# Hybrid decoder trunk on one core: the MLP's up and down products issued in pairs of one kind

## The chip, the cores and the metric

The kernel runs on one core of one Trainium2 chip. The time is that of one execution on the device, in microseconds; lower is better. The core has a matrix engine (TensorE, PE in the profile, with its weight loads shown apart as PEld), three engines for elementwise work (VectorE or DVE, ScalarE or ACT, GpSimd or POOL) and a queue that starts transfers (SyncE, SP). TensorE writes its results to PSUM, eight banks of 128 x 512 floats here, from which DVE and ACT read them.

## The reference

Two layers on a residual stream of 512 tokens by 1024, in float32. The first has a latent attention, the second a gated linear attention, and each is followed by an MLP:

```python
def sq_relu_mlp(xn, w_up, w_down):
    hid = jnp.square(jax.nn.relu(xn @ w_up))
    return hid @ w_down

def reference(x, ...):
    for i in range(DEPTH):              # DEPTH = 2
        xn = rms_norm(x, norm_mix[i])
        ...                             # mixer
        x = x + mix.astype(x.dtype)
        x = x + sq_relu_mlp(rms_norm(x, norm_mlp[i]), mlp_w_up[i], mlp_w_down[i]).astype(x.dtype)
    return rms_norm(x, final_norm)
```

`w_up` is 1024 x 4096, `w_down` 4096 x 1024. Only the MLP is touched by the change.

## The kernel before

Each float32 operand is split into a high part, which ACT copies, and a low part, which DVE subtracts; a product is then three matmuls (high by high, high by low, low by high). The split of a weight piece of 128 x 1024 is `piece`: `wh` on ACT (L104), `wl` on DVE (L107). There are four rooms for `wh` and four for `wl`, so a piece is split at the earliest when the product four places before it has left its room.

`mlp` walks over the 4096 hidden columns in eight blocks of 512. Its first up block is done plainly (`up_first`); then come seven calls of `step(b)`, b = 0 to 6, and the last down block stands behind them. A step multiplies down block b and up block b+1, both by a scheme with seven products of half-size blocks in place of eight (sums of quadrants are formed before and after). So a step has seven up products and seven down products:

- an up product (`up_product`, matmuls on L946) is 24 matmuls, each with a 128 x 128 block of split weights held in the array and 256 columns of activations moving; it writes one bank of the tag `u` (four of them: `z`, `y`, `w`, `w2`);
- a down product (`down_product`, matmuls on L955) is 12 matmuls, each with a 128 x 128 block of activations held and 512 columns of weights moving; it writes two banks, `d` or `e`, of which there is one pair each.

Up products are named by their quadrant: 11, 21, T2, T1, 22, T3, T4. In before, they alternate with the down products: up 11, down `d11`, up 21, down `d12`, up T2, down `d11` (changed in place by `ds1`, against -q11), up T1, down `d12` (changed in place), up 22, down `ds3`, up T3, down `ds1`, up T4, down `d22`.

Around the products stand the sums. ACT copies a bank into another as the start of the next sum (`begun`, L964; L976 and L978 in `onto`), DVE adds banks to totals (L1000, L971), and `finish` squares the hidden values of the next block (DVE L849, ACT L850). The quadrants q11, q12, q21, q22 are changed in place on DVE (L1002, L1003, L1034, L1045).

Weights come by DMA. `fetch` starts the transfer of the next block's piece as soon as `after(name)` is called, that is when this block's piece of that room has been used: `A1` and `A2` are the up pieces (1 MB each, rooms `wraw`, started on SP at L134), `S1`, `dS1`, `dS3`, `d11`, `d12`, `d22` the others (rooms `comb`, L933). A second transfer from POOL's queue adds a further quadrant to `S1`, `dS1`, `dS3` and `A2` (L935, L925). A transfer waits on its queue until the room is free, and those behind it wait with it.

The framework's scheduler turns the program into one row of instructions per engine. On PE that row follows the program's order in all steps but b = 0, and ACT, DVE and SP follow it with small shifts.

Of the kernel before, what the change touches and what calls it, by code (L numbers as in the profile page):

```python
# [14 lines left out]
AF = mybir.ActivationFunctionType  # L15
ALU = mybir.AluOpType
# [34 lines left out]
def trunk_kernel(ctx: ExitStack, tc: tile.TileContext, t_in: dict, out: bass.AP):  # L51
    nc = tc.nc
    PE, ACT, DVE, POOL, SP = nc.tensor, nc.scalar, nc.vector, nc.gpsimd, nc.sync
# [5 lines left out]
    def uname(s):  # L59
        count[0] += 1  # L60
        return f"{s}_{count[0]}"
# [14 lines left out]
    def bank(tag):  # L76
        return psum["pool"].tile([P, 512], F32, tag=f"ps_{tag}", bufs=psum["banks"][tag], name=uname("ps"))

    def two_banks(tag):
        return psum["pool"].tile([P, 1024], F32, tag=f"ps_{tag}", bufs=1, name=uname("ps2"))  # L80

    def split_banks(tag):
        t = two_banks(tag)
        return [t[:, :512], t[:, 512:]]
# [4 lines left out]
    def tmp(shape=(P, 512), dt=F32):  # L89
        return sb.tile(list(shape), dt, tag="tmp", bufs=6, name=uname("tmp"))  # L90
# [11 lines left out]
    def split(src, hi, lo, hi_eng=ACT, lo_eng=DVE, order=lambda i: i):  # L102
        if hi_eng is ACT:
            order(ACT.activation(hi, src, AF.Copy))  # L104
        else:
            hi_eng.tensor_copy(hi, src)
        lo_eng.tensor_tensor(lo, src, f(hi), ALU.subtract)  # L107
# [35 lines left out]
    def piece(raw, a, n, order=lambda i: i, at=W_AT):  # L143
        hi = room_for("wh", a, n, at)
        lo = room_for("wl", a, n, at)
        split(raw, hi, lo, order=order)
        return hi, lo

    def cut(pair, *idx):
        return tuple(t[idx] for t in pair)  # L150
# [654 lines left out]
    def mlp(layer, nrm, nxt=None):  # L805
        w_up, w_dn = t_in["mlp_w_up"][layer], t_in["mlp_w_down"][layer]
        X = nrm.out
        NB = FF // FB
# [13 lines left out]
        S11, S12, SU, S21, S5 = sums  # L822
# [7 lines left out]
        def by_tile(v):  # L830
            return v.rearrange("p (j t) -> p j t", j=2)

        def signed(src, hi, lo, sign):
            ACT.activation(hi, src, AF.Copy, scale=sign)
            DVE.scalar_tensor_tensor(lo, src, sign, f(hi), ALU.mult, ALU.subtract)

        def parts_of_quad(src, sign=1.0):
            hi, lo = parts_room[turn[0] % 4]
            turn[0] += 1
            if sign == 1.0:  # L840
                split(src, hi, lo)
            else:
                signed(src, hi, lo, sign)
            return hi, lo

        def finish(src, half, th, q):
            r = tmp()
            r_t = nrm.rstd[:, (first, second)[th]].unsqueeze(1).to_broadcast([P, 2, TH])
            DVE.scalar_tensor_tensor(by_tile(r), by_tile(src), 0.0, r_t, ALU.min if half else ALU.max, ALU.mult)  # L849
            ACT.activation(q[half][th], r, AF.Square)  # L850
# [87 lines left out]
        def up_product(t, a, q, start):  # L938
            w = piece(a, KH, 256, at=W_AT_UP)
            for j in range(2):  # L940
                o = t[:, j * TH : (j + 1) * TH]
                for k in range(KH):
                    wh, wl = cut(w, slice(None), k, slice(j * P, (j + 1) * P))
                    xh, xl = quad[q][k][:, 0], quad[q][k][:, 1]
                    for n, (a_, x_) in enumerate(((wh, xh), (wh, xl), (wl, xh))):
                        PE.matmul(o, a_, x_, start=start and j == 0 and k == 0 and n == 0, stop=k == KH - 1 and n == 2, skip_group_check=True)  # L946

        def down_product(t, a, parts, start):
            wh, wl = piece(a, 2, 512)
            for tt in range(2):  # L950
                o = t[:, tt * 512 : (tt + 1) * 512]
                for k in range(2):
                    xh, xl = cut(parts, slice(None), slice(k * TH + tt * P, k * TH + (tt + 1) * P))
                    for n, (x_, w_) in enumerate(((xh, wh[:, k]), (xh, wl[:, k]), (xl, wh[:, k]))):
                        PE.matmul(o, x_, w_, start=start and k == 0 and n == 0, stop=k == 1 and n == 2, skip_group_check=True)  # L955


        def step(b, q, r, after):
            opening = b == 0 and nxt is not None
            (q11, q12), (q21, q22) = q  # L960

            def begun(src):
                t = two_banks("e")
                ACT.activation(t, src, AF.Copy)  # L964
                return t

            def add(total, t):
                if opening:
                    ACT.activation(total, t, AF.Copy)
                else:  # L970
                    DVE.tensor_tensor(total, t, total, ALU.add)  # L971

            def onto(tag, total, a, parts, fresh=False):
                t = two_banks(tag)
                if not fresh:
                    ACT.activation(t, total, AF.Copy)  # L976
                down_product(t, a, parts, fresh)
                ACT.activation(total, t, AF.Copy)  # L978

            A1, A2, s1 = W["A1"], W["A2"], W["S1"]  # L980
            a11, a12, s3, a22 = A1[:, :KH], A1[:, KH:], A2[:, :KH], A2[:, KH:]
            d11, d12, ds1, ds3, d22 = (W[n] for n in ("d11", "d12", "dS1", "dS3", "d22"))

            z = bank("u")
            up_product(z, a11, "11", True)
            y = bank("u")
            ACT.activation(y, z, AF.Copy)

            d = two_banks("d")
            down_product(d, d11, parts_of_quad(q11), True)  # L990
            if opening:
                ACT.activation(S11, d, AF.Copy)
            e = two_banks("e") if opening else begun(d)

            up_product(y, a12, "21", False)
            finish(y, 0, 0, r)
            DVE.tensor_tensor(a11, s1, a11, ALU.add)

            down_product(e, d12, parts_of_quad(q21), opening)
            DVE.tensor_tensor(S11, e, S11, ALU.add)  # L1000
            DVE.tensor_tensor(d11, ds1, d11, ALU.add)
            DVE.tensor_tensor(q12, q22, q12, ALU.subtract)  # L1002
            DVE.tensor_tensor(q11, q11, q12, ALU.add)  # L1003

            up_product(z, a11, "T2", False)
            u = tmp()
            ACT.activation(u, z, AF.Copy)
            DVE.tensor_tensor(a12, a11, a12, ALU.add)

            down_product(d, d11, parts_of_quad(q11, -1.0), False)  # L1010
            e = begun(d)
            DVE.tensor_tensor(d12, d11, d12, ALU.add)
            after("d11")

            w = bank("u")
            up_product(w, s1, "T1", True)
            w2 = bank("u")
            ACT.activation(w2, w, AF.Copy)
            after("S1")

            down_product(e, d12, parts_of_quad(q22), False)
            add(S12, e)
            after("d12")

            up_product(w, a12, "22", False)
            c = tmp()
            DVE.tensor_tensor(c, w, u, ALU.add)
            finish(c, 0, 1, r)
            after("A1")

            down_product(d, ds3, parts_of_quad(q12), False)
            add(SU, d)
            after("dS3")
            DVE.tensor_tensor(q22, q22, q11, ALU.subtract)  # L1034

            up_product(z, s3, "T3", False)
            v = tmp()
            ACT.activation(v, z, AF.Copy)
            c = tmp()
            DVE.tensor_tensor(c, w2, v, ALU.add)  # L1040
            finish(c, 1, 1, r)

            onto("e", S5, ds1, parts_of_quad(q22, -1.0), b == 0)
            after("dS1")
            DVE.tensor_tensor(q21, q21, q11, ALU.subtract)  # L1045

            up_product(z, a22, "T4", False)
            finish(z, 1, 0, r)
            after("A2")

            onto("d", S21, d22, parts_of_quad(q21, -1.0), opening)
            after("d22")

        up_first(Q[0])
        quadrants()
# [45 lines left out]
        for b in range(NB - 1):  # L1101
# [3 lines left out]
            def after(name, b=b, final=final, old=old):  # L1105
                if final:
                    return before_next(name) if nxt else at_the_end(name)
                new = NEXT[name]
                if name in home:
                    home[new] = old[name]  # L1110
                fetch(b + 1, new)
# [4 lines left out]
        if nxt:  # L1116
# [6 lines left out]
            for c in range(2):  # L1123
                if c == 0:
                    ps_ = [bank("u") for _ in range(4)]
                else:
                    e, d = split_banks("e"), split_banks("d")
# [6 lines left out]
                for j, p in enumerate(ps_):  # L1134
                    if j % 2 == 0:
                        w = piece(last_raw[c][:, :, j * P : (j + 2) * P], 4, 256)
# [524 lines left out]
    for k0, k1 in ((0, 1), (1, 2), (2, 4), (4, 6), (6, 8)):  # L1661
        w = piece(raw0[:, k0:k1], k1 - k0, KL, tc.keep_in_program_order)
# [9 lines left out]
    O, begun = mla(0, nrm, w0, mla_pools)  # L1672
# [23 lines left out]
    Y, begun = gla(0, n_mix1, "B", "B")  # L1696
# [54 lines left out]
```

## Time and profile before

| what | value |
|---|---|
| runs shown, median of 3 | 1054.07 us (1053.84 to 1054.35) |
| profiled execution | 1054.16 us |
| its span, first to last instruction | 1052.4 us |
| TensorE busy | 1043.0 us (99%) |
| VectorE busy | 874.2 us (83%) |
| ScalarE busy | 702.6 us (67%) |
| granted TensorE clock | 0.999 |

A profile row of an instruction gives its start and length in us (the length runs to the end of the last matmul of a group, and neighbouring matmuls overlap in the pipe, so the rate of PE is read from the distance of the starts), then the engine, the line, the operation, what it writes and reads with the sizes, and how many are taken together. In brackets stands how long the engine was idle before it and who ended that. The chain of waits goes back from the last instruction to what released each one.

### The profile page before, as it was taken

The numbers are of one execution on the slowest core, as the hardware profiler recorded it, in microseconds if no ns is written. First come the engines' busy times: TensorE is split into PE (matmuls) and PEld (weight loads), VectorE is DVE, ScalarE is ACT, GpSimd is POOL, SyncE is SP. The second block draws the span as 40 slices with busy tenths as digits, with TensorE's granted clock in tenths as the row PEclk, the third lists the DMA queues.
The fourth block names the chain that finished last, engine by engine and source line by source line (L and its number), as shares of the span: only waits on it lengthen the run. The fifth ranks groups of instructions, "written<-read, shape, count | busy, mean of one in ns | idle before, by whom it ended". The sixth has DMA issues, their size and how long they took to land.

```text
span 1052.4 us, 15648 instructions
## 1 busy us (share of the span) xinstructions
PE 1043.0 (99%) x5966; PEld 910.3 (86%) x5966; DVE 874.2 (83%) x1340; ACT 702.6 (67%) x1074; POOL 113.8 (11%) x128
## 2 busy tenths in 40 slices
PE   9999999999999999999999999999999999999997
PEld 7788888899999999998888888888889999999985
DVE  7889977979889889988687399469889989989983
ACT  8667654677777777776445565555667777777784
POOL 7400010301101011000000000000010010110000
PEclk9999999999999999999999999999999999999999
DMA  7401234776975875843212222164496696696612
GB/s 232 121 21 41 81 100 141 236 189 147 230 198 141 222 214 134 214 160 121 70 62 80 90 72 78 46 161 154 96 249 135 185 247 144 178 244 158 172 61 80
DMA packets 120492, 149.97 MB, mean 143 GB/s; under 512 B 9344, under 2 KB 86144, under 8 KB 120288
## 3 DMA queue, kind: packets, MB, share of 16 engines
q1 hardware_dynamic: 95920, 117.76, 35.3%
q0 software_dynamic: 22400, 29.36, 17.2%
q10 hardware_dynamic: 2096, 1.84, 0.6%
q8 instruction: 47, 0.77, 0.3%
q14 instruction: 29, 0.24, 0.1%
HBM read 144.49 MB, written 4.19 MB: 141 GB/s over the span
## 4 chain that ended last, share of the span: by engine, by line
PE 93%; DVE 3%; ACT 2%; DMA 1%; issue 1%; ACTq 0%; SPq 0%; DVEq 0%
PE ps L955 26%; PE ps L946 26%; PE ps L112 10%; PE ps L114 10%; PE ps L113 10%; PE ps L1140 2%; PE ps L1395 1%; PE ps L129 1%; PE ps L1175 1%; PE ps L414 1%; PE ps L1522 1%; DVE wl L107 1%; DVE acc L245 0%; PE ps L1445 0%; PE ps L677 0%
## 5 line engine op out<-in xcount | busy, mean ns | idle before, releaser
L955 PE MATMUL ps<-wh,set 128*128 128x512 f32 x784 | 259.2, 392 | 0.1
L104 ACT ACTIVATE wh<-wraw 128x1024 fp32r<-128x1024 f32 x139 | 147.0, 1061 | 115.2 <-PE ps L946 40.0
L107 DVE TENSOR_TENSOR wl<-wraw,wh 128x1024 fp32r<-128x1024 f32 x139 | 169.9, 1222 | 40.7 <-ACT wh L104 40.3
L955 PEld LDWEIGHTS ps<-wh,set 128*128 128x128 f32 x784 | 147.1, 188 | 29.3 <-ACT set L104 0.5
L946 PE MATMUL ps<-T,wh 128*128 128x256 f32 x896 | 159.8, 279 | 0.0
L107 DVE TENSOR_TENSOR wl<-comb,wh 128x1024 fp32r<-128x1024 f32 x112 | 136.6, 1219 | 22.8 <-ACT wh L104 22.8
L955 PE MATMUL ps<-wl,set 128*128 128x512 f32 x392 | 153.7, 392 | 0.0
L946 PEld LDWEIGHTS ps<-T,wh 128*128 128x128 f32 x896 | 140.4, 188 | 4.7
L104 ACT ACTIVATE wh<-comb 128x1024 fp32r<-128x1024 f32 x112 | 117.7, 1051 | 25.0 <-PE ps L955 15.0
L946 PE MATMUL ps<-T,wl 128*128 128x256 f32 x448 | 124.9, 279 | 0.0
L946 PE MATMUL ps<-set,wh 128*128 128x256 f32 x672 | 119.7, 280 | 0.0
L112 PE MATMUL ps<-set,wh 128*128 128x512 f32 x280 | 109.2, 391 | 0.5 <-ACT set L1564 0.3
L113 PE MATMUL ps<-set,wh 128*128 128x512 f32 x280 | 109.5, 391 | 0.0
L114 PE MATMUL ps<-set,wl 128*128 128x512 f32 x280 | 109.2, 390 | 0.0
L946 PEld LDWEIGHTS ps<-set,wh 128*128 128x128 f32 x672 | 105.2, 188 | 3.5
L946 PE MATMUL ps<-set,wl 128*128 128x256 f32 x336 | 93.8, 279 | 0.0
L946 PEld LDWEIGHTS ps<-T,wl 128*128 128x128 f32 x448 | 84.2, 188 | 0.1
L955 PEld LDWEIGHTS ps<-wl,set 128*128 128x128 f32 x392 | 73.6, 188 | 11.7
L935 POOL DMA_DIRECT2D comb<-in_mlp_w_down_dram x28 | 33.8, 1207 | 387.9 <-DMA comb<-in_mlp_w_down_dram 271.5
L946 PEld LDWEIGHTS ps<-set,wl 128*128 128x128 f32 x336 | 63.2, 188 | 0.0
L112 PEld LDWEIGHTS ps<-set,wh 128*128 128x128 f32 x280 | 52.5, 188 | 11.6 <-issue 0.6
L114 PEld LDWEIGHTS ps<-set,wl 128*128 128x128 f32 x280 | 52.6, 188 | 10.8
(396 smaller groups left out, 2026.1 us busy)
## 6 DMA issues: line engine op xcount, KB each, us to landing
comb<-in_mlp_w_down_dram SPq DMA_DIRECT2D x74, 512.0 KB, 5.6
wraw<-in_mlp_w_up_dram SPq DMA_DIRECT2D x32, 1024.0 KB, 7.0
comb<-in_mlp_w_down_dram POOLq DMA_DIRECT2D x28, 512.0 KB, 7.6
wraw<-in_gla_w_in_dram SPq DMA_DIRECT2D x12, 1024.0 KB, 5.2
comb<-in_mlp_w_up_dram SPq DMA_DIRECT2D x14, 512.0 KB, 4.4
comb<-in_mlp_w_up_dram POOLq DMA_DIRECT2D x14, 512.0 KB, 10.7
wraw<-in_mlp_w_up_dram POOLq DMA_DIRECT2D x14, 512.0 KB, 6.5
wraw<-in_mla_w_o_dram SPq DMA_DIRECT2D x4, 1024.0 KB, 4.9
```

Of the source, the lines that this page charges most:

```text
L104: order(ACT.activation(hi, src, AF.Copy))
L107: lo_eng.tensor_tensor(lo, src, f(hi), ALU.subtract)
L112: PE.matmul(psum, wh, xh, start=start, stop=False)
L113: PE.matmul(psum, wh, xl, start=False, stop=False)
L114: PE.matmul(psum, wl, xh, start=False, stop=stop)
L129: PE.transpose(psum, src, ident[: src.shape[0], : src.shape[0]])
L414: PE.matmul(p, w[:, i, j * P : (j + 1) * P], x, start=start, stop=stop)
L935: POOL.dma_start(t, q(b, *more), accum_op=ALU.add)
L946: PE.matmul(o, a_, x_, start=start and j == 0 and k == 0 and n == 0, stop=k == KH - 1 and n == 2, skip_group_check=True)
L955: PE.matmul(o, x_, w_, start=start and k == 0 and n == 0, stop=k == 1 and n == 2, skip_group_check=True)
L1140: PE.matmul(p, a, x, start=False, stop=k == 3 and n == 2, skip_group_check=True)
L1175: PE.matmul(o, a, b_, start=False, stop=k == 3 and n == 2, skip_group_check=True)
```

## The change

The products of `step` become small functions, and a table sets the order in which they are called. In step b = 0 the order stays as it was. In the others the two products behind up 11, down `d11`, up 21 and down `d12` change places (`d11` again, then T2), likewise 22 and `ds3`, and, in steps 1 to 5, T4 and `d22`. A step's pattern is then up, down, up, two down, two up, two down, two up, two down, up, and the next step begins with an up product. In the last step (b = 6) it ends T4, `d22`, as before. What a product computes and which copies and sums go with it is unchanged.

```diff
-            up_product(z, a11, "T2", False)
-            u = tmp()
-            ACT.activation(u, z, AF.Copy)
-            DVE.tensor_tensor(a12, a11, a12, ALU.add)
-
-            down_product(d, d11, parts_of_quad(q11, -1.0), False)
-            e = begun(d)
-            DVE.tensor_tensor(d12, d11, d12, ALU.add)
-            after("d11")
...
+            part = {"e": e}
+
+            def down_11():
+                down_product(d, d11, parts_of_quad(q11, -1.0), False)
+                part["e"] = begun(d)
+                DVE.tensor_tensor(d12, d11, d12, ALU.add)
+                after("d11")
+
+            def up_t2():
+                up_product(z, a11, "T2", False)
+                u = part["u"] = tmp()
+                ACT.activation(u, z, AF.Copy)
+                DVE.tensor_tensor(a12, a11, a12, ALU.add)
...
+            if b == 0:
+                order = up_t2, down_11, up_t1, down_22, up_22, down_12, up_t3
+            else:
+                order = down_11, up_t2, up_t1, down_22, down_12, up_22, up_t3
+            ends = (up_t4, down_21) if b in (0, NB - 2) else (down_21, up_t4)
+            for product in (*order, down_5, *ends):
+                product()
```

The first place is PE's row in step b = 4 of the second layer, where the second down product ends. `ps_1577` is the bank pair `e`, `ps_1574` the pair `d`, `ps_9102` the bank `z`, `T` the parts of T2. Before:

```order
L955 MATMUL ps_1577_9152<-wh_9188,set_7290 128x512
L955 MATMUL ps_1577_9152<-wl_9189,set_7290 128x512
L955 MATMUL ps_1577_9152<-wh_9188,set_7291 128x512
L946 MATMUL ps_9102<-T_1342_7471,wh_9208 128x256 x2
L946 MATMUL ps_9102<-T_1342_7471,wl_9209 128x256
```

And with the change:

```order
L955 MATMUL ps_1577_9152<-wh_9188,set_7290 128x512
L955 MATMUL ps_1577_9152<-wl_9189,set_7290 128x512
L955 MATMUL ps_1577_9152<-wh_9188,set_7291 128x512
L955 MATMUL ps_1574_9133<-wh_9210,set_7292 128x512
L955 MATMUL ps_1574_9133<-wl_9211,set_7292 128x512
```

Behind the down product on `e` now stands the one on `d`, and T2 comes after it.

The second place is ACT's row at the same point: `wh` of a `comb` belongs to a down product or to T1 (`comb_8904`), `wh` of a `wraw` to an up product, L964 is `begun`, `set` are halves of quadrants. Before:

```order
L104 ACTIVATE wh_9208<-wraw_8961 128x1024
L987 ACTIVATE ps_9131<-ps_9102 128x512
L834 ACTIVATE set_7292<-set_7280 128x512
L104 ACTIVATE set_7288<-set_7281 128x512
L964 ACTIVATE ps_1577_9152<-ps_1574_9133 128x1024
L104 ACTIVATE wh_9241<-comb_8926 128x1024
L104 ACTIVATE wh_9264<-comb_8904 128x1024
```

With the change:

```order
L987 ACTIVATE ps_9131<-ps_9102 128x512
L104 ACTIVATE wh_9210<-comb_8926 128x1024
L104 ACTIVATE set_7288<-set_7281 128x512
L964 ACTIVATE ps_1577_9152<-ps_1574_9133 128x1024
L104 ACTIVATE wh_9232<-wraw_8983 128x1024
L104 ACTIVATE wh_9264<-comb_8904 128x1024
```

The split for the second use of `d11` (`comb_8926`) moves ahead of `begun`, and that of T2 (`wraw`) behind it.

The third place is SP's row of transfers in step b = 5 of the second layer, from `dS1` to the last. Before:

```order
L933 DMA comb_9650<-in_mlp_w_down_dram 128x2x512
L933 DMA comb_9684<-in_mlp_w_up_dram 128x4x256
L933 DMA comb_9706<-in_mlp_w_down_dram 128x2x512
L134 DMA wraw_9741<-in_mlp_w_up_dram 128x8x256
L933 DMA comb_9762<-in_mlp_w_down_dram 128x2x512
L933 DMA comb_9821<-in_mlp_w_down_dram 128x2x512
L134 DMA wraw_9856<-in_mlp_w_up_dram 128x8x256
L933 DMA comb_9880<-in_mlp_w_down_dram 128x2x512
```

With the change:

```order
L933 DMA comb_9619<-in_mlp_w_down_dram 128x2x512
L933 DMA comb_9684<-in_mlp_w_up_dram 128x4x256
L933 DMA comb_9706<-in_mlp_w_down_dram 128x2x512
L933 DMA comb_9727<-in_mlp_w_down_dram 128x2x512
L134 DMA wraw_9763<-in_mlp_w_up_dram 128x8x256
L933 DMA comb_9821<-in_mlp_w_down_dram 128x2x512
L933 DMA comb_9846<-in_mlp_w_down_dram 128x2x512
L134 DMA wraw_9879<-in_mlp_w_up_dram 128x8x256
```

`A1` (the first `wraw`) moves behind `d12`, and `A2` (the second) behind `d22`.

More of the change, by code (lines that the diff above doesn't have):

```diff
@@ L1003, in step @@
             DVE.tensor_tensor(q11, q11, q12, ALU.add)
-            up_product(z, a11, "T2", False)
-            u = tmp()
-            ACT.activation(u, z, AF.Copy)
-            DVE.tensor_tensor(a12, a11, a12, ALU.add)
-            down_product(d, d11, parts_of_quad(q11, -1.0), False)
-            e = begun(d)
-            DVE.tensor_tensor(d12, d11, d12, ALU.add)
-            after("d11")
[L1015 to L1052, printed above, removed]
+            part = {"e": e}
@@ new lines, in down_11, with up_t1 @@
+            def down_11():
[8 more added lines that the diff above has]
+                DVE.tensor_tensor(a12, a11, a12, ALU.add)
+            def up_t1():
+                w = part["w"] = bank("u")
+                up_product(w, s1, "T1", True)
+                w2 = part["w2"] = bank("u")
+                ACT.activation(w2, w, AF.Copy)
+                after("S1")
@@ new lines, in down_22, with down_12, up_22 @@
+            def down_22():
+                e = part["e"]
+                down_product(e, d12, parts_of_quad(q22), False)
+                add(S12, e)
+                after("d12")
+            def down_12():
+                down_product(d, ds3, parts_of_quad(q12), False)
+                add(SU, d)
+                after("dS3")
+                DVE.tensor_tensor(q22, q22, q11, ALU.subtract)
+            def up_22():
+                w = part["w"]
+                up_product(w, a12, "22", False)
+                c = tmp()
+                DVE.tensor_tensor(c, w, part["u"], ALU.add)
+                finish(c, 0, 1, r)
+                after("A1")
@@ new lines, in up_t3, with down_5, down_21 @@
+            def up_t3():
+                up_product(z, s3, "T3", False)
+                v = tmp()
+                ACT.activation(v, z, AF.Copy)
+                c = tmp()
+                DVE.tensor_tensor(c, part["w2"], v, ALU.add)
+                finish(c, 1, 1, r)
+            def down_5():
+                onto("e", S5, ds1, parts_of_quad(q22, -1.0), b == 0)
+                after("dS1")
+                DVE.tensor_tensor(q21, q21, q11, ALU.subtract)
+            def down_21():
+                onto("d", S21, d22, parts_of_quad(q21, -1.0), opening)
+                after("d22")
@@ new lines, in up_t4 @@
+            def up_t4():
+                up_product(z, a22, "T4", False)
+                finish(z, 1, 0, r)
+                after("A2")
+            if b == 0:
[5 more added lines that the diff above has]
+                product()
```

## The prediction

> **What bounds the kernel now.** I read first the head of the page, then the chain that ended last, then single instructions around the products. The page's head and its first and fourth part:
>
> ```profile
> span 1052.4 us, 15648 instructions
> PE 1043.0 (99%) x5966; PEld 910.3 (86%) x5966; DVE 874.2 (83%) x1340; ACT 702.6 (67%) x1074; POOL 113.8 (11%) x128
> PE 93%; DVE 3%; ACT 2%; DMA 1%; issue 1%; ACTq 0%; SPq 0%; DVEq 0%
> PE ps L955 26%; PE ps L946 26%; PE ps L112 10%; PE ps L114 10%; PE ps L113 10%; PE ps L1140 2%; PE ps L1395 1%; PE ps L129 1%; PE ps L1175 1%; PE ps L414 1%; PE ps L1522 1%; DVE wl L107 1%; DVE acc L245 0%; PE ps L1445 0%; PE ps L677 0%
> ```
>
> TensorE is the chain for 93% of the span, and half of the span is the two lines that the change reorders, L946 (up products) and L955 (down products). A busy PE may still hide gaps, so I look at the chain in order of time in the second layer's steps (start, length, what):
>
> ```profile
> 768.40 2.80 PE ps L946 x24
> 771.20 2.75 PE ps L955 x12
> ...
> 1018.30 2.80 PE ps L946 x24
> 1021.10 2.75 PE ps L955 x12
> ```
>
> From 768.40 to 1018.30 lie 45 pairs of one up and one down product: 249.90 / 45 = 5.553 us each, and every pair shows the same 2.80 + 2.75. PE never waits here for data, and the first layer's steps read alike. So reordering can remove no wait; it can only change what a product costs on PE, or make a wait.
>
> **What a turn from up to down costs.** One down product between two up products, matmul by matmul (start, length):
>
> ```profile
> 776.59 0.40 PE L955 MATMUL ps<-wh,set 128*128 128x512 f32 x1
> 777.75 0.61 PE L955 MATMUL ps<-wh,set 128*128 128x512 f32 x2
> 779.11 0.40 PE L955 MATMUL ps<-wh,set 128*128 128x512 f32 x1
> 779.34 0.40 PE L946 MATMUL ps<-T,wh 128*128 128x256 f32 x2
> ```
>
> Its first five matmuls run from 776.59 to 777.75, 232 ns apiece. The next six run to 779.11, 1.36 / 6 = 227 ns. To the next up product the last one takes 0.23. The trace also holds one place, in the first layer's opening step, where two down products follow each other, 22 matmuls without an up product between:
>
> ```profile
> 218.52 0.65 PE L955 MATMUL ps<-wh,set 128*128 128x512 f32 x2
> 219.01 0.39 PE L955 MATMUL ps<-wl,set 128*128 128x512 f32 x1
> 223.31 0.40 PE L955 MATMUL ps<-wh,set 128*128 128x512 f32 x1
> 223.55 0.40 PE L946 MATMUL ps<-T,wh 128*128 128x256 f32 x2
> ```
>
> From the third to the twenty-second are 19 steps in 4.30 us: 226.3 ns apiece, straight through the border between the two products. So the second of two neighbouring down products should take 12 x 0.2266 = 2.72 us (226.6 is the middle of the two readings, 226.3 and 227), where a lone one takes 2.75: 0.03 us less, with stamps that are rounded to 0.01. Put together from its parts the excess is 5 x 5.4 ns at the start and some 7 at the end (0.23 to 0.24 against 0.227), 0.034 us. That is what each up-down alternation that goes is worth, if an up product costs 2.80 behind another one too; in the steady pairs its 24 matmuls go at 117 ns from the first to the last, so I know of no excess that it could lose.
>
> **The change part by part.** It removes no instruction and adds none. The runs of down products number 98 in the order of before and 64 in the new one: in each layer, steps 1 to 5 go from seven runs to four (the last up product joins the next step's first), step 6 from seven to five, step 0 stays. That is 2 x (5 x 3 + 2) = 34 alternations. 34 x 0.034 = 1.16 us, the one term with a gain.
>
> The bounds of this term: the 0.034 could belong to the start of each product rather than to the turn, and then nothing is saved (0). Or a turn could cost more after two up products than after one. The chain has the double run in both layers:
>
> ```profile
> 218.69 5.03 PE ps L955 x22
> 763.33 5.07 PE ps L955 x22
> ```
>
> So the same turn can cost 0.04 us more or less by what went before it. With turns at 0.034 + 0.04 a step would cost 4 x 0.074 - 7 x 0.034 = 0.058 us more, over twelve steps 0.7 us; with turns dearer today than the double run shows, the gain could be 34 x 0.05 = 1.7 us at most. I take 1.16, because the double run shows the border itself.
>
> **What hides the splits.** Each product needs its weights split first, `wh` on ACT and `wl` on DVE, in four rooms each. DVE is the fuller of the two. One step of the second layer, the busy time of PE, PEld, DVE, ACT and POOL in 38.8 us with PE's clock, the DMA share and GB/s behind it, and the waits in all steps of that layer (us in total, times, longest):
>
> ```profile
> 888.90:927.70 38.80, 38.80 (x254) 35.30 (x253) 34.77 (x38) 28.63 (x36) 5.02 (x4) 1.00 0.76 190
> ```
>
> ```profile
> ACT wh L104 <- PE ps L946: 20.8, 35, 1.6
> DVE wl L107 <- ACT wh L104: 18.6, 24, 1.8
> ```
>
> DVE has 4 us of slack in a step, and the two waits say that ACT and DVE run ahead until PE gives a room back (and DVE behind ACT). The tightest place of a step is its second down product; DVE, then PE (three products):
>
> ```profile
> 910.13 1.21 DVE L107 TENSOR_TENSOR wl<-comb,wh 128x1024 fp32r<-128x1024 f32 x1
> 911.87 1.22 DVE L107 TENSOR_TENSOR wl<-wraw,wh 128x1024 fp32r<-128x1024 f32 x1
> 913.01 0.68 DVE L835 SCALAR_TENSOR_TENSOR set<-set,set 128x512 fp32r<-128x512 f32 x1
> 915.35 1.22 DVE L107 TENSOR_TENSOR wl<-comb,wh 128x1024 fp32r<-128x1024 f32 x1
> 918.82 1.21 DVE L1000 TENSOR_TENSOR xT<-ps,xT 128x1024 f32<-128x1024 f32 x1
> ```
>
> ```profile
> 915.42 0.40 PE L955 MATMUL ps<-wh,set 128*128 128x512 f32 x1
> 918.17 0.40 PE L946 MATMUL ps<-T,wh 128*128 128x256 f32 x2
> 920.97 0.40 PE L955 MATMUL ps<-wh,set 128*128 128x512 f32 x1
> ```
>
> Its `wl` ends at 911.34, 4.08 us ahead of 915.42. The next two are the pair that the change swaps (T2 and the second use of `d11`). Today T2's `wl` ends at 913.09 for 918.17 (5.08 ahead), the other at 916.57 for 920.97 (4.40 ahead). In the new order, which front shows on ACT, the down product's split takes T2's place and T2's the other's: 5.08 us ahead of 918.17, and 916.57 against 918.17 + 2.75 = 920.92, 4.35 us ahead. The low half of -q11 (0.68 us at 913.01) must be done ahead of the down product too, and 5.08 us hold it. The same reckoning for the other two swaps (U22 with the `dS3` product; T4 with `d22`) moves a lead by the difference of 2.80 and 2.75. New is that DVE's work comes in lumps: a down product asks it for a `wl` (1.22), a half of a quadrant (0.68), a bank to add (1.21) and a sum of quadrants (0.68), 3.8 us, so a pair asks for 2 x 3.8 - 5.5 = 2.1 us more than its own time on PE, which the up products around it give back. From 4.08 that leaves a lead of 2.0 us, and I cost the splits at nothing; without this cover each us would be paid in each step. PSUM: the one copy that is tight, `begun(d)`, feeds the second down product, whose place does not move.
>
> **DMA.** SP fetches in the order of the releases. The change puts `d12`'s fetch ahead of A1's and `d22`'s ahead of A2's (front shows the rows); POOL's adding transfers keep their order, that of `dS1` can start a product sooner and that of A2 a product later. A2 and the down pieces are read eight and more products after their fetch. A1 (1 MB) is read first thing in the next step. Its issue waits for the `wl` of U22, which now takes the place of the one behind it (DVE, today's two). Then SP, the landing of that one issue, that of all such issues in the second layer, and the reader's side (ACT, DVE, PE):
>
> ```profile
> 922.29 1.21 DVE L107 TENSOR_TENSOR wl<-wraw,wh 128x1024 fp32r<-128x1024 f32 x1
> 926.29 1.23 DVE L107 TENSOR_TENSOR wl<-comb,wh 128x1024 fp32r<-128x1024 f32 x1 [1.19 <-ACT wh L104]
> ```
>
> ```profile
> 923.53 0.37 SPq L134 DMA_DIRECT2D wraw<-in_mlp_w_up_dram  x1
> ```
>
> ```profile
> wraw<-in_mlp_w_up_dram SPq DMA_DIRECT2D x1, 1024.0 KB, 11.7
> ```
>
> ```profile
> DMA to landing us min/median/max: 6.1/7.5/12.3
> ```
>
> ```profile
> 937.77 1.06 ACT L104 ACTIVATE wh<-wraw 128x1024 fp32r<-128x1024 f32 x1 [0.45 <-PE ps L946]
> 938.73 0.58 ACT L1038 ACTIVATE tmp<-ps 128x512 f32<-128x512 f32 x1
> ```
>
> ```profile
> 938.86 1.23 DVE L107 TENSOR_TENSOR wl<-wraw,wh 128x1024 fp32r<-128x1024 f32 x1 [1.46 <-ACT wh L104]
> ```
>
> ```profile
> 943.19 0.40 PE L955 MATMUL ps<-wh,set 128*128 128x512 f32 x1
> 945.94 0.40 PE L946 MATMUL ps<-set,wh 128*128 128x256 f32 x2
> ```
>
> Today it lands at 935.2, 2.5 us before ACT turns to it. Issued behind the later split, at 926.29 + 1.23 = 927.5, it would land at 939.2: ACT waits 1.4 us. The product itself starts at 945.94 and its `wl` (today ended at 940.1) would end at 941.5, still 4.4 us ahead. Queued behind on ACT is the copy of T3's bank (0.58), which T4 needs; T4 is now the last product (today's starts at 943.19). So the cover is gone when the landing takes over 943.1 - 0.58 - 1.06 - 927.5 = 14.0 us; the longest seen is 12.3. Price: nothing.
>
> **Sum.** The profiled execution took 1054.16 us for a span of 1052.4, 1.76 us around it, and the median of the runs is 1054.07. 1054.16 - 1.16 = 1053.0, and by the median 1052.9 us. That is 0.11% below; what a measurement of this kernel can tell from no change is about 0.2%, 2.1 us.
>
> **The rivals.** (a) The 34 ns belong to each product: nothing changes, 1054.1, or up to 0.7 above if the turn after two up products is dearer. For it: every lone down product has them and only one double run is seen. Against it: that run. (b) A stall in the new place, slower: A1 late. If landings stretch past 14.0 us, because `d12`'s fetch now goes ahead of A1 on the same queue, each us beyond it stops PE for as long, at the end of five steps of each layer. At 15 us that is 10 x 1.0 = 10 us: 1063; at 14.4 us 4 us, 1057. For it: 11.7 us is already slow, and the queue is full there (DMA's share of the step is 0.76). Against: the 0.5 MB put ahead of A1 are in flight today beside it, the total is the same. (c) Runs of one kind go at the bare rate of the columns, without what each matmul pays now. The rows make that part 6.8 ns: an up matmul's 256 columns take 2.80 / 24 = 116.7 ns, a down matmul's further 256 columns 226.6 - 116.7 = 109.9. A second down product at 2 x 109.9 per matmul would take 2.64 us, the gain would be 34 x 0.115 = 3.9 us, the time 1050.2. For it: only that such a part exists; against: the double run, which stays at 226.3.
>
> The Trainium skill (TensorE: Matmul & The Clock Gate, section Back-to-back issue gap) goes the same way as (c): it gives 512 / 2.4 + 2.5, about 216 ns, for the isolated gap of a 512-column matmul at full clock. By that figure, as an estimate, the change would bring 34 x 0.16 = 5.4 us. The double run of this trace, at 226.3 ns, does not agree.
>
> That the new order is not what the text says is excluded, for the order of PE's rows shows it.
>
> **How the numbers follow.** Forecast 0.66, own range 1052.5 to 1053.5. (a) 0.14, 1053.6 to 1054.8. (b) 0.13, from 1055 up. (c) 0.07. The range 1052.2 to 1054.9 holds the first two, 0.80. Faster by over 0.2% needs 1051.96 or less: (c), 0.07. Slower by over 0.2%, above 1056.2: nearly all of (b), 0.12. In between lies 0.81.
>
> **What would show it.** Right: in the chain of the new profile a pair of down products at 5.47 to 5.48 us (x24) and a pair of up products at 5.60; no wait of PE on L946 or L955 in the steps. Wrong in its gain: pairs of 5.51. Wrong in its covers: gaps before a step's first or last up product with ACT or the DMA of `wraw` as releaser, or a `wl` that ends less than 1 us before its product.

## The result, and the profile after

Over 17 runs of each kernel the change takes 1052.81 us (median; 1052.07 to 1053.5) and before 1054.24 us. The ratio is 0.9987 with a 95% interval of 0.9981 to 0.9993: faster by 0.13%, 1.4 us, less than the 0.2% set as the line in the prediction, though its interval leaves out 1.

The page of the profiled execution of the change (1052.22 us), the rows that answer to those of before:

```profile
span 1050.5 us, 15642 instructions
PE 1041.6 (99%) x5966; PEld 910.1 (87%) x5966; DVE 874.3 (83%) x1340; ACT 699.5 (67%) x1074; POOL 113.8 (11%) x128
PE 94%; DVE 3%; ACT 2%; issue 1%; DMA 0%; ACTq 0%; SPq 0%; DVEq 0%
```

PE is still the chain; the number of instructions on each engine is the same, and PE's busy time is 1.4 us less. The chain in order of time, second layer (start, length, what):

```profile
886.40 5.47 PE ps L955 x24
891.87 5.60 PE ps L946 x48
897.47 5.47 PE ps L955 x24
902.94 5.60 PE ps L946 x48
908.54 2.75 PE ps L955 x12
911.29 2.80 PE ps L946 x24
914.10 5.47 PE ps L955 x24
```

To the hundredth, two up products take twice what one takes (5.60 and 2.80). Two down products take 5.47 where one takes 2.75: the second costs 2.72. Nothing waits between them. One such pair in single matmuls, PE (four of its rows):

```profile
886.23 0.40 PE L955 MATMUL ps<-wh,set 128*128 128x512 f32 x1
887.39 0.62 PE L955 MATMUL ps<-wh,set 128*128 128x512 f32 x2
891.47 0.40 PE L955 MATMUL ps<-wh,set 128*128 128x512 f32 x1
891.71 0.40 PE L946 MATMUL ps<-set,wh 128*128 128x256 f32 x2
```

The first five take 1.16 us, 232 ns apiece, once per pair. The next 18 take 4.08 us, 226.7 ns apiece, and the border between the products (886.23 + 2.75 = 888.98) lies among them.

Where the time went is told by stretches of PE's starts: from the first up product to the first matmul behind the last step of each layer, and what lies around. The step column is the length of a step in the middle of a layer, start of its first matmul to that of the next step's.

| kernel | to the first up product | MLP 1 | between | MLP 2 | last rows and tail | a middle step |
|---|---|---|---|---|---|---|
| before | 206.61 | 272.39 | 270.17 | 274.51 | 28.69 | 38.873 |
| the change | 206.01 | 271.83 | 270.18 | 273.90 | 28.58 | 38.773 |

The two MLP stretches give 0.56 + 0.61 = 1.17 us, a middle step 0.100. The 0.60 us in the first stretch are the start of two single executions (see the next run).

### The profile page after: what moved, and what is told of

The parts are those of the page before. It is cut to its first block, busy times and chain, and to the rows that moved or that the text cites. A ratio compares the mean times of both kernels' runs of the same rounds, so it can differ in the third digit from the quotient of the medians.

```text
span 1050.5 us, 15642 instructions
## 1 busy us (share of the span) xinstructions
PE 1041.6 (99%) x5966; PEld 910.1 (87%) x5966; DVE 874.3 (83%) x1340; ACT 699.5 (67%) x1074; POOL 113.8 (11%) x128
## 4 chain that ended last, share of the span: by engine, by line
PE 94%; DVE 3%; ACT 2%; issue 1%; DMA 0%; ACTq 0%; SPq 0%; DVEq 0%
PE ps L946 26%; PE ps L955 26%; PE ps L112 10%; PE ps L114 10%; PE ps L113 10%; PE ps L1162 2%; PE ps L1417 1%; PE ps L129 1%; PE ps L1197 1%; PE ps L414 1%; PE ps L1544 1%; DVE wl L107 1%; DVE acc L245 0%; PE ps L1681 0%; PE ps L1467 0%
## 5 line engine op out<-in xcount | busy, mean ns | idle before, releaser
L955 PE MATMUL ps<-wh,set 128*128 128x512 f32 x784 | 252.9, 391 | 0.1
L112 PEld LDWEIGHTS ps<-set,wh 128*128 128x128 f32 x280 | 52.5, 188 | 11.7 <-issue 0.6
```

Of the source, the lines that this page charges most:

```text
L112: PE.matmul(psum, wh, xh, start=start, stop=False)
```

## The experiments

**Before once more.** No edit.

> The kernel before, once more, for the spread of single stretches from one execution to the next. Between the two profiles the stretch up to the first up product differed by 0.59 us, though the change does not touch it. If that is chance, this run's stretch lies anywhere from 205.9 to 206.8 us, while its two MLP stretches (first up product to the first matmul behind the last step) repeat at 272.39 and 274.51 us within 0.05. If the 0.59 us come from the change, the first stretch is 206.6 again.

The one run took 1053.79 us. The first stretch took 206.30 us, the MLP stretches 272.41 and 274.50, a step 38.873 to 38.874. So the first stretch moves by some tenths from one execution to the next (206.0 to 207.2 over the eleven profiles of this study, and the change touches nothing ahead of its end), while the MLP stretches repeat within 0.02 us and their middle steps within 0.001. Step 0 is the least steady part: the first layer's took 39.15 to 39.19 us in the profiles of the kernels that leave it as it was and do not hold A1 back. The stretches measure far more finely than the whole time does, and the runs below are read by them.

**One swap alone.** In steps 1 to 6 the order is that of before but for `d11`, T2:

```diff
-                order = down_11, up_t2, up_t1, down_22, down_12, up_22, up_t3
+                order = down_11, up_t2, up_t1, down_22, up_22, down_12, up_t3
-            ends = (up_t4, down_21) if b in (0, NB - 2) else (down_21, up_t4)
+            ends = up_t4, down_21
```

> One of the three swaps alone (the second use of d11 ahead of T2, in steps 1 to 6). 86 runs of down products. Theory: 12 turns fewer, the MLP stretches shrink by 12 x 0.0344 = 0.41 us together against before (0.21 each). Rival (the gain sits in the other two swaps, by what they do to ACT, DVE or the fetches): no gain here.

The one run took 1053.11 us. The MLP stretches took 272.22 and 274.31 us, 0.38 us less than before together; a step 38.840, 0.033 less. One turn fewer per step brings a third of what three bring (0.100). The gain goes by the count of turns.

**More turns.** The order of before, with four of the seven down products cut in half in steps 1 to 6. The first half is issued in the middle of the up product ahead of it:

```diff
             for j in range(2):
+                if j and mid:
+                    mid.pop()()
...
+            def pre_11():
+                halves["11"] = down_halves(d, d11, parts_of_quad(q11, -1.0), False)
+                halves["11"](0)
...
+                for up, pre, post in ((up_t2, pre_11, post_11), (up_t1, None, down_22), (up_22, pre_12, post_12), (up_t3, pre_5, post_5), (up_t4, pre_21, post_21)):
+                    if pre:
+                        mid.append(pre)
+                    up()
+                    post()
```

> More turns instead of fewer: the order of before, but in steps 1 to 6 the first half of four of the seven down products stands in the middle of the up product ahead of it. 146 runs of down products instead of 98. Theory (each turn costs 0.035 us): the two MLP stretches grow by 48 x 0.035 = 1.7 us together against before, in halves of 6 down matmuls that keep the slow first five and the dear last one; the time goes to about 1055.8. Rival (the 0.035 us belong to each product, whatever stands beside it): the MLP stretches stay at 272.39 and 274.51. Rival (splits too late, for each down product is asked for 1.4 us sooner): waits of PE on L955, over 0.1 us apiece.

The time was 1058.49 us, a ratio of 1.0040 to before (1.0026 to 1.0054), and the MLP stretches 274.38 and 276.58: 4.05 us more, not 1.7. A step took 39.207, 0.334 more, of which four turns at 0.0334 are 0.134. The other 0.200 stand at one place in each step. PE, then ACT, where T4 begins (rows picked out; T4 is L950 in this kernel, the halves L965; L1060 is the copy of T3's bank):

```profile
903.20 0.40 PE L965 MATMUL ps<-wh,set 128*128 128x512 f32 x1
904.36 0.61 PE L965 MATMUL ps<-wh,set 128*128 128x512 f32 x2
904.94 0.50 PE L950 MATMUL ps<-T,wh 128*128 128x256 f32 x2
905.27 0.28 PE L950 MATMUL ps<-T,wl 128*128 128x256 f32 x1
```

```profile
904.30 0.58 ACT L1060 ACTIVATE tmp<-ps 128x512 f32<-128x512 f32 x1
```

The copy ends at 904.88 and T4's first matmul starts at 904.94, 0.58 us behind the start of the last two of the half product, which take 0.47 in the halves of the next run; its first two then take 0.33 us in place of 0.24. Between T3 and T4 stands only half a down product of 1.4 us here, in place of a whole one of 2.75. In the list of waits such a gap of 0.1 to 0.2 us hardly shows, because the matmuls overlap in the pipe; the starts show it.

**More turns, without that wait.** T3 and its down product stand whole again:

```diff
-                (up_t3, pre_5, post_5)
+                (up_t3, None, down_5)
```

> The kernel of e1_split, but T3 and the dS1 product stand whole, so that the copy of T3's bank has a whole down product to hide behind again. 134 runs of down products, 36 more than before. Theory (a turn costs 0.0334 us, as the steps of the change and of e2_one_swap give it, and what e1_split lost beyond that was the wait of T4 for that copy): steps 1 to 5 take 38.873 + 3 x 0.0334 = 38.973 us, both MLP stretches together 36 x 0.0334 = 1.2 us more than before, the time some 1055.4. Rival (splitting a down product costs more by itself, in each of the four places of e1_split): steps 1 to 5 take 38.873 + 0.75 x 0.333 = 39.12 us.

A step took 38.973 us, the MLP stretches 273.02 and 275.09: 1.21 us more for 36 turns. The ratio to before is 1.0014 (1.0005 to 1.0024), the time 1055.62. The chain, where L950 is up and L965 down:

```profile
881.74 1.39 PE ps L965 x6
883.13 1.40 PE ps L950 x12
884.53 1.39 PE ps L965 x6
885.93 2.80 PE ps L950 x24
888.73 2.75 PE ps L965 x12
```

Half a down product takes 1.39 to 1.40, not 2.75 / 2: each half pays the start and the end in full. The cost is that of the turn, not of the product, and it can be added as well as taken away.

**The down matmuls made narrow.** The order of before, each down matmul of 512 columns as two of 256:

```diff
-                        PE.matmul(o, x_, w_, start=start and k == 0 and n == 0, ...)
+                        for c in (0, 256):
+                            PE.matmul(o[:, c : c + 256], x_, w_[:, c : c + 256], start=start and k == 0 and n == 0 and c == 0, ...)
```

> The order of before, with each down matmul of 512 columns split into two of 256, so that a down product is 24 matmuls of 256 columns like an up product. The result stays the same. Theory A (the turn's cost comes from the change of width between up and down matmuls): a down product now takes what an up product takes, 2.80 us, without slow first matmuls, and a step 14 x 2.799 = 39.18 us. Theory B (it comes from the change of what is held and what moves, weights or activations, or from the border of products as such): the first matmuls behind a turn stay slower and a step takes 39.18 + 7 x 0.033 = 39.42 us.

Neither number came: a step took 39.760 us (the one run 1066.92). The chain (L956 is the narrow down product):

```profile
894.50 2.81 PE ps L946 x24
897.30 2.87 PE ps L956 x24
900.18 2.81 PE ps L946 x24
902.98 2.87 PE ps L956 x24
```

A narrow down matmul takes 2.87 / 24 = 120 ns where an up matmul takes 117, and that is 0.5 of the 0.6 us over theory A. No slow beginning is seen, though. In the same kernel the first four matmuls of a down product and the four behind them, PE:

```profile
902.82 0.40 PE L956 MATMUL ps<-wh,set 128*128 128x256 f32 x2
903.30 0.64 PE L956 MATMUL ps<-wh,set 128*128 128x256 f32 x4
903.78 0.40 PE L956 MATMUL ps<-wl,set 128*128 128x256 f32 x2
```

902.82 to 903.30 and 903.30 to 903.78 are 0.48 us each. What is held and what moves still changes at each turn here, and the slow start does not come. That speaks for theory A but does not settle it: a pair of narrow matmuls takes 240 ns, more than the 232 of a slow wide one, so a slow start could be hidden under that pace. The profile of before has other borders that bear on it. The last 512-column matmul ahead of a layer's first up product holds weights as the up product does, and is dear all the same (206.37 to 206.61, 0.24 us against 0.227): at the end of a run the width alone is enough. And the slow start also comes without a change of width, at one matmul that reads 96 rows in place of 128 (PE, three of the rows):

```profile
528.19 0.40 PE L1338 MATMUL ps<-tmp,tmp 96*128 96x512 f32 x1
529.13 0.39 PE L112 MATMUL ps<-set,wh 128*128 128x512 f32 x1
530.03 0.39 PE L113 MATMUL ps<-set,wh 128*128 128x512 f32 x1
```

The first four matmuls take 0.94 us, the next four 0.90. As far as these rows show it, the slow start goes with a change of shape, of which the width is one case; why the array takes up to five matmuls to reach its pace, no run here shows.

**Step 0 paired too.**

```diff
-            if b == 0:
-                order = up_t2, down_11, up_t1, down_22, up_22, down_12, up_t3
-            else:
-                order = down_11, up_t2, up_t1, down_22, down_12, up_22, up_t3
-            ends = (up_t4, down_21) if b in (0, NB - 2) else (down_21, up_t4)
+            order = down_11, up_t2, up_t1, down_22, down_12, up_22, up_t3
+            ends = (up_t4, down_21) if b == NB - 2 else (down_21, up_t4)
```

> The paired order and the new end in step 0 too. 60 runs of down products instead of the change's 64. Theory (turns alone): 0.14 us less than the change over both layers. Rival (step 0 starts starved, its splits and quadrant sums come late, and a pair needs two down splits at once): PE waits longer in step 0 and the MLP stretches grow by 0.3 to 2 us each.

The rival came: the MLP stretches took 272.34 and 274.41 us, 0.51 more than the change in each layer, all of it in step 0 (39.67 against 39.15 us in the first layer). The time was 1054.00 us, a ratio to before of 0.9997 (0.9987 to 1.0006). Its waits of PE (us in total, times, longest) have a row that the change's list lacks:

```profile
PE ps L946 <- DVE wl L107: 1.2, 2, 0.6
```

The product that waits is T2. Its split now comes one place later on ACT and DVE, behind that of the second use of `d11`, while PE's row in step 0 still has it right behind up 21; its low part ends at 216.09 us and the matmul that needs it starts at 216.14. PE loses 0.6 us there in each layer against turns worth 0.1.

**The last step paired too.**

```diff
-            ends = (up_t4, down_21) if b in (0, NB - 2) else (down_21, up_t4)
+            ends = (up_t4, down_21) if b == 0 else (down_21, up_t4)
```

> The change with the new end (d22 ahead of T4) in the last step of each layer too. 62 runs of down products. Theory (turns alone): 0.07 us less than the change. Rival (what stands behind the last step needs T4's result: finish, square and split take 0.68 + 0.63 + 0.63 + 0.68 us and some latency, 3.2 us in all, against 1.65 us of transposes and 1.4 us of matmuls on the other halves in the first layer): PE waits 0.1 to 0.5 us there, and about nothing in the second layer, where that half is read after 5 us of other rows; the time stays the change's within 0.4 us.

1053.40 us, a ratio to before of 0.9994 (0.9985 to 1.0004), which does not tell it from the change. The stretches do: the MLP takes what it takes with the change (271.84 and 273.89; without step 0, which scatters, 0.02 to 0.03 us less, so the turn may be there), but 270.49 stand between the layers, 0.31 more. The chain there, behind the first layer's last step (L849 is `finish`, L1155 the transposes behind the step):

```profile
478.47 1.14 DVE wl L107
479.61 0.61 DVE tmp L849
480.26 0.66 PE ps L1155 x4
```

The wait of 0.3 us has the size that was expected, but not the place. It is not the split of T4's result that is late: the last four transposes wait for `finish`, which reads T4's bank and stands behind other work on DVE.

**A1 later.** The change, with A1's fetch held on SP behind another; `who` is `dS1` (the fetch of `dS3`) in the first run and `d22` in the second:

```diff
+                if name == "A1":
+                    return
                 new = NEXT[name]
...
-                fetch(b + 1, new)
+                first_part = fetch(b + 1, new)
+                if name == who:
+                    with tc.issue_after(first_part.ins):
+                        fetch(b + 1, "A1")
```

> The change, with A1's fetch held behind that of dS3 on SP, in steps 0 to 5 of both layers: issued some 6 us later than with the change (at 931.3 on its clock instead of 925.3). With a landing of 8 to 9 us it is there at 939.3 to 940.3, where ACT has turned to it at 936.2. Theory (the cover ends with the copy of T3's bank that is queued behind A1's split on ACT and that T4 waits for, at a landing of 939.9): PE waits 0 to 0.5 us at T4 in each of 12 steps, 0 to 6 us in all. Rival (A1's fetch is on the path already): 3 to 4 us in each step, some 40 us in all. Rival (A1 does not matter at all): nothing.

> The same, with A1's fetch behind that of d22: issued at 933.9, landed at 942 to 943. Theory: T4, which would start at 941.6, waits for the copy behind A1's split until 943.7 to 944.7, so 2 to 3 us in each of 12 steps, 25 to 37 us in all, and the wait stands ahead of L946 with ACT's copy as the releaser. Rival (only A1's own product waits, and ACT's queue does not matter): its weights are split at 944.5 to 945.5 for a start at 944.4, so 0.1 to 1.1 us in each step, 2 to 13 us in all, ahead of the step's first up product.

One run each: 1060.12 and 1073.58 us. The MLP stretches grew against the change by 6.6 us (1.4 and 5.2) and by 20.1 (7.4 and 12.7). The sizes lie just over the upper end of what was expected and between the two theories; the place was named wrong. The scheduler had moved the copy of T3's bank (L1049) ahead of A1's split in both kernels, so T4 never waited for it. PE's waits in the first kernel, then in the second:

```profile
PE ps L946 <- ACT ps L987: 2.4, 4, 1.1
PE ps L955 <- ACT xT L978: 1.7, 2, 1.5
```

```profile
PE ps L946 <- ACT wh L104: 7.8, 2, 4.7
PE ps L946 <- DVE wl L107: 2.5, 5, 0.8
```

Counted from each step's first product, the first kernel issues A1 6 to 8 us later than the change does in steps 1 to 5, and 8 to 9 later in step 0. What is queued behind its split on ACT comes late first: the copy that up 21 adds to (L987), and the copy out of `d` (L978), which the next step's first down product overwrites.

The second kernel issues it 8 to 12 us later in steps 1 to 5, but 13 to 15 later in step 0. There the edit does more than delay: step 0 ends T4, `d22`, so the fetch of A2 is now called ahead of that of A1 and takes its place: it is issued 17.75 us behind the step's first product, where the change issues A1. SP, POOL (whose adding transfer L925 belongs to A2 alone), then SP again:

```profile
224.64 0.37 SPq L134 DMA_DIRECT2D wraw<-in_mlp_w_up_dram  x1
```

```profile
235.32 1.29 POOL L925 DMA_DIRECT2D wraw<-in_mlp_w_up_dram  x1 [10.83 <-DVE wl L107]
```

```profile
239.35 0.52 SPq L134 DMA_DIRECT2D wraw<-in_mlp_w_up_dram  x1
```

The first transfer is A2, the last is A1. The two long waits of A1's own product (4.7 us in the first layer, 3.1 in the second) are those at the end of step 0. About the end of each, the profile shows the granted clock fall to 0.50 and stay there for 6.8 us. The stretch in the first layer (PE, PEld, DVE, ACT and POOL busy, then PE's clock, the DMA share and GB/s), and two of PE's rows in it:

```profile
248.50:255.30 6.80, 3.91 (x16) 3.61 (x17) 4.35 (x4) 5.32 (x6) 0.00 (x0) 0.50 0.01 3
```

```profile
253.00 0.41 PE L946 MATMUL ps<-set,wl 128*128 128x256 f32 x1
253.64 0.42 PE L946 MATMUL ps<-set,wl 128*128 128x256 f32 x1
```

Three up matmuls take 0.64 us, 213 ns apiece in place of 117. In both layers 38 up matmuls (96 ns more each) and 4 down ones (200 ns more) start at that clock: some 4.5 of the 20.1 us, an estimate, are the clock and not a wait. In the first kernel the longest gap between two starts on PE was 1.8 us, and the clock stayed at 1.00. The loss differs from step to step (0 to 2.0 us in the first kernel; in the second 4.9 in the first layer's step 0, 2.5 in step 1, of which 1.5 are the clock, and in its steps 2 to 6 none). What sets the rest of that pattern was not settled.

## Why the prediction was right

**The bound.** From step 1 on no product waited on data before, and none does after; step 0, left as it was, takes 0.28 us more than a steady step of before in the first layer's profile of either kernel. The change could win only what a product costs on PE, and that is where all of the settled gain lies.

**The cost of a turn, 0.034 us.** Measured 0.0333 (0.100 for three turns in a step, 0.033 for one taken away alone, 0.100 for three added). By PE's starts in the second layer's steps of the change a pair of down products takes 0.035 us less than two lone ones, and a pair of up products 0.002 more, for the last matmul ahead of a down product (113 ns, in place of 118) comes once less. The predicted pairs, 5.47 to 5.48 and 5.60, are in the chain. Rival (a), that the cost belongs to the product, fell with the one swap and with the halves. Rival (c), the bare column rate, fell too: the second down product runs at 226.7 ns a matmul, not at 219.8.

**The count, 34, and the sum, 1.16 us.** The MLP stretches are 1.17 us shorter. The two medians are 1.43 us apart, with 0.7 to 2.0 in the interval; the rest is within what the first and last stretches vary.

**The splits.** The price, nothing, was right, and one of the two leads was close: T2's 4.35 us was 4.31. The second use of `d11` was put at 5.08 and had 4.46. The rows of the change, DVE, then PE (T2; the second use of `d11` starts at 913.93 + 2.75 = 916.68):

```profile
911.01 1.21 DVE L107 TENSOR_TENSOR wl<-comb,wh 128x1024 fp32r<-128x1024 f32 x1
913.88 1.22 DVE L107 TENSOR_TENSOR wl<-wraw,wh 128x1024 fp32r<-128x1024 f32 x1
```

```profile
913.93 0.40 PE L955 MATMUL ps<-wh,set 128*128 128x512 f32 x1
919.41 0.40 PE L946 MATMUL ps<-T,wh 128*128 128x256 f32 x2
```

The term for DVE's lumps was too dark: it left 2.0 us, and the least lead in the second layer's last five steps is 4.11 (before 4.07). It also moved: the second down product, tightest before, has 5.18 us, and up 21 now has the least. That the pair's extra work is spread over the products around it is the likely reason; no run here tests it.

**A1.** The price, nothing, was right, but its working was not. SP, the landing of that issue, and the ACT row that reads it:

```profile
925.34 0.37 SPq L134 DMA_DIRECT2D wraw<-in_mlp_w_up_dram  x1
```

```profile
wraw<-in_mlp_w_up_dram SPq DMA_DIRECT2D x1, 1024.0 KB, 8.0
```

```profile
936.22 1.06 ACT L104 ACTIVATE wh<-wraw 128x1024 fp32r<-128x1024 f32 x1 [0.65 <-PE ps L946]
```

Counted from the step's first product the issue comes 3.3 us later than before (4.0 was said), but the landing takes 8.0 us in place of 11.7, so A1 is there at 933.3, 2.9 us before ACT turns to it. That landing is no exception: in the second layer's steps 1 to 5 A1 took 7.9 to 8.3 us, before 11.3 to 12.3. The prediction carried the old landing over, though the transfers around it had moved as well; that these make the difference was not tested. The limit of 14.0 us was also built on one order of ACT's row; the two late runs show that other copies give way first. Rival (b) is real as a mechanism: with A1 issued 6 us and more later than the change issues it, PE waits. No shorter delay was run, so where the waits begin is not shown.

**The parts left out.** Why step 0 and the last step keep their ends was not asked in the prediction. The two runs show it: pairing step 0 costs 0.5 us per layer, and the last step's new end 0.3 us behind the first layer.

## What to carry to other kernels

When one engine is full and never waits, look at the starts of its instructions and not at its idle time: a cost of 0.03 us per change of shape hides in "99% busy", and it can be counted before anything is built. Such a gain goes by the number of changes, so a run with more of them tests it as well as one with fewer. The stretch between two marks on the full engine repeated within some hundredths of a microsecond here, where whole executions scatter by 1 us; measure small changes there. And when a transfer is moved to test a limit, look in the profile at what took its place, and at the granted clock, before the loss is put down to waiting.

## What the runs showed of the hardware

A stream of 512-column matmuls that follows 256-column ones goes at 232 ns for its first five and then at 226.7, and its last one ahead of a narrow one takes 235. With narrow matmuls on both sides no slow start is seen, at a pace of 120 ns that could hide it; a single matmul of 96 rows among 512-column ones of 128 brings a slow start too. A matmul of 256 columns took 120 ns in narrow pairs that hold the same activations, against 117 in the up products. A 1 MB fetch took 3.7 us less to land (8.0 against 11.7) when it was issued 3.3 us later, behind other transfers. With gaps of 5.1 and 3.5 us between two starts on PE the granted clock fell to 0.50 for 6.8 us, and a 256-column matmul took 213 ns; with gaps of up to 1.8 us it did not fall.
